# First layer: modulation weights worked feature by feature, with the first three projection tiles accumulated alongside

## The chip, the cores and the metric

One core of a Trainium2 chip runs the whole program; the other cores are idle. The number that counts is the device time of one execution in microseconds. PE is TensorE (matmuls), DVE is VectorE, ACT is ScalarE, POOL is GpSimd, and SP issues most of the loads. Each engine works through its own list of instructions in order and waits for the others by semaphores, so an instruction that waits holds up everything behind it on its engine.

## What is computed

Two layers of a diffusion backbone on 256 latent and 256 context tokens, 1024 features wide. Cut to the part that the change touches:

```python
silu_c, silu_cc = silu(c), silu(c_ctx)                 # conditioning vectors, 1024 each
for l in range(2):
    mx = silu_c @ w_ada[l] + b_ada[l]                  # (6 * 1024): shift, scale, gate, twice
    mc = silu_cc @ w_ada[l] + b_ada[l]                 # the same for the context tokens
    sh1, sc1, ga1, sh2, sc2, ga2 = split(mx, 6)
    ux = (rmsnorm(x, g_mix[l]) * (1 + sc1) + sh1) @ w_in[l]
    # uc the same from ctx and mc; then four token mixers, one output projection,
    # x = x + ga1 * (...), and a second modulated norm with a SwiGLU (layer 1: 8 experts)
```

The change is in the opening of layer 0: how `sh1` and `sc1` (the first 2048 of the 6144 modulation features, from an 8 MB slice of `w_ada[0]`) are made, and when the projection by `w_in[0]` begins.

## The kernel before, in words

Activations lie with features on the partitions: `xt[k]` is feature tile k (128 features) by 512 tokens (256 latent, 256 context). The program runs in stages. They are an opening, the mixer of layer 0 (projections, then attention and two other mixers, then the output projection `w_out`), a dense feed-forward, the mixer of layer 1 and the experts.

**Opening.** `ada_first` (L166 to L193) loads the 8 MB slice as 16 tiles of 512 KB, each 128 of the 1024 inputs by 1024 of the 2048 outputs. Every output needs all inputs, so two accumulators (`pss`) take 64 small matmuls (L179, 32 rows by 256 columns, the operand being silu of the two conditioning vectors), and no feature is known before the last tile is in. Between them stand the loads of `xt`, their squares and sum (`add_sq`, tile `sm`), and `spread` (L195), which copies the conditioning vectors over all partitions (tile `scb`) by 16 matmuls on 16 little tiles that DVE makes. `inv_rms` turns `sm` into the reciprocal norms `rs`, which stay in a PSUM tile of the pair named S. Then four transposes (L189) bring the features onto partitions, as `mod[0]`.

**Modulated input.** `modulated` (L269) makes `A` (gain times one plus scale) for all tiles at once, and then for each k: DVE makes `ht`, ACT the rounded high part `hh[k]` (L286) and the shifted sum (L288, second half of the tokens), DVE and POOL the low part `hl[k]` (L291 and L289).

**Projections.** Each product is three matmuls per feature tile, L135 to L137: high by high, low by high, high by low, 24 for one output tile of 512 columns. The weights come through `pump` (L97): a `raw` load on SP, the high part on ACT (L102), the low part alternately on POOL and DVE (L104). Twelve projections (`proj`) and a transposed pair make the mixer's inputs; three PSUM accumulators named acc rotate among them, and one is free again when ACT has copied and squared what is in it.

**Columns.** The other 4096 features of layer 0, and all of layer 1, come otherwise: `more(n)` takes n columns `ar` (512 KB, two buffers) and DVE multiplies each by `scb` and sums it, once per conditioning vector (L227). `more` is called after every `proj` with the number of its output tiles, twice in the transposed pair, and once in each of four attention calls. `w_out` (L557) then works off what is missing: it may begin its first tile only with at most 62 of the 80 columns left, and it ends only with 56 left, since the dense stage needs those.

The order on each engine is set by a scheduler that goes by readiness; the columns' instructions keep the order of the program among themselves (`pinned`).

Of the kernel before, what the change touches and what calls it, by code (L numbers as in the profile page):

```python
# [52 lines left out]
def backbone(ctx: ExitStack, tc: tile.TileContext, a: dict, out: bass.AP, dbg=None):  # L53
# [10 lines left out]
    def acc(w=512):  # L64
        return psp.tile([128, 512], F32, name="acc", bufs=3)[:, :w]
# [98 lines left out]
    def ada_first():  # L164

        pss = [acc(256) for _ in range(2)]  # L166
        sm = per.tile([128, T], F32, name="sm", bufs=2)
        for k in range(KT):
            if k == 2:
                spread()  # L170
            for hf in range(2):
                if 2 <= k < 6:
                    i = 2 * k + hf - 4
                    sp.dma_start(xt[i], a["xt"][i])
                    add_sq(sm, i, T)
                r = wa.tile([128, 1024], F32, name="wa", bufs=6)
                sp.dma_start(r, a["wa0"][k, hf])
                for g in range(4):
                    pe.matmul(pss[hf][32 * g:32 * g + 32], scv[:, k, :], r[:, 256 * g:256 * g + 256],  # L179
                              start=k == 0, stop=k == KT - 1)  # L180
            if k == 5:
                table(AF.Sqrt, sm)
        rs = at_once(inv_rms(sm, T, 128, D))
        for hf in range(2):
            ev = per.tile([128, T], F32, name="sq", bufs=2)[:, :256]
            (dve.tensor_copy if hf else act.copy)(ev, pss[hf])
            for c in range(2):
                pm = psp.tile([128, 512], F32, name="T", bufs=2)[:, :128]
                pe.transpose(pm, ev[:, 128 * c:128 * c + 128], C("ident"))  # L189
                m = mod[0][:, 8 * hf + c:8 * hf + 8:2]  # L190
                bias = V(0, "b_ada", 8 * hf, 8)[:, c::2]
                dve.tensor_add(m, pm.rearrange("p (g z) -> p g z", g=4)[:, :, :2], bias[:, :, None].to_broadcast([128, 4, 2]))
        return rs  # L193
# [75 lines left out]
    def modulated(l, gname, jsh, jsc, tmp, w, sm, emit, then=None, rs=None, nt=3):  # L269
        A = tmp.tile([128, KT, 2], F32, name="A")  # L270
        for s in range(w // 256):
            dve.scalar_tensor_tensor(A[:, :, s], mod[l][:, jsc:jsc + KT, s], 1.0, V(l, gname, 0, 8), op0=ALU.add, op1=ALU.mult)
        if rs is None:
            rs = at_once(inv_rms(sm[:, :w], w, 128, D))
        if then:
            table(then, rs)
        for k in range(KT):
            t = tmp.tile([128, T], F32, name="ht", bufs=nt)
            for s in range(w // 256):
                c = slice(256 * s, 256 * s + 256)  # L280
                dve.scalar_tensor_tensor(t[:, c], xt[k][:, c], A[:, k, s:s + 1], rs[:, c], op0=ALU.mult, op1=ALU.mult)
                emit(k, s, c, t, mod[l][:, jsh + k, s:s + 1])

# [10 lines left out]
    def mixer(l, sm, oh, ol, rs=None):  # L294
# [5 lines left out]
        mx = ctx2.enter_context(sb(f"mx{l}"))  # L300
        qh = [mx.tile([96, nx], F32, name=f"qh{h}") for h in range(4)]
        kh = [mx.tile([96, T], F32, name=f"kh{h}") for h in range(4)]
        nq = [mx.tile([128, nx], F32, name=f"nq{h}") for h in range(2)]
        nk = [mx.tile([128, T], F32, name=f"nk{h}") for h in range(2)]
        vv = mx.tile([128, 4, 256], F32, name="vv")
        nv = mx.tile([128, 4, 256], F32, name="nv")
        rf = [mx.tile([128, nx], F32, name=f"rf{i}") for i in range(2)]
        rp = [mx.tile([128, nx], F32, name=f"rp{i}") for i in range(2)]
        nb = mx.tile([128, 2, 4, 256], F32, name="nb")
        swb = mx.tile([128, 768], F32, name="swb")  # L310
        cstc = mx.tile([128, 1280], F32, name="cstc")
        wf = swb[:, :512].rearrange("p (k c) -> p k c", k=2)
        wp = swb[:, 512:].rearrange("p (k c) -> p k c", k=2)
        g8 = mx.tile([128, 1], F32, name="g8")
        dve.tensor_scalar(g8, V(l, "g_naq"), 0.125, None, op0=ALU.mult)
        with sb(f"hp{l}", "right") as hp:
# [7 lines left out]
            pump(2 if last else 3)  # L324
# [4 lines left out]
            modulated(l, "g_mix", 0, 8, hp, T, sm, emit, None, rs, nt)  # L329
# [95 lines left out]
            p, p1 = proj(2, T)  # L425
            spawn(keys(p))
            spawn(rope(p1, T, V(l, "g_kr"), kh))
            spawn(queries(proj(2, nx)))
# [919 lines left out]
    act.activation(scv[:, :, :2], cv, AF.Silu)  # L1348
    rxp = None
# [10 lines left out]
    with ExitStack() as early:  # L1360
        adp = early.enter_context(sb("adp"))
        with sb("wa", "right") as wa:
            rs = ada_first()
        pump(0)
        with ExitStack() as ctx2:
            sm = mixer(0, None, None, None, rs)
# [80 lines left out]
def _layout(i):  # L1447
# [8 lines left out]
    d["wa0"] = wa[0, :, :2048].reshape(KT, 128, 2, 1024).transpose(0, 2, 1, 3)  # L1456
# [78 lines left out]
```

## Time and profile before

| | |
|---|---|
| three runs | 1800.61, 1801.84, 1802.29 us (median 1801.84) |
| profiled execution | 1801.68 us, of which 1799.9 us span |
| PE busy | 1638.6 us, 91% of the span |
| DVE busy | 831.1 us, 46% |
| ACT busy | 573.8 us, 32% |
| POOL busy | 384.0 us, 21% |
| HBM read | 472.76 MB, 263 GB/s over the span |
| mean granted PE clock | 0.954 of full speed |

The busy shares are averages over stages with different limits, so they do not tell what a change in the opening is worth. For that one reads the opening, the projections and `w_out` one by one: which engine works in each, and which wait ends last. PE's busy time is modelled to the end of each pipelined matmul; the distance from one start to the next says how fast it really goes.

### The profile page before, as it was taken

The page shows a single profiled execution, that of the slowest core. Times are in us where ns is not written, and L with a number is a line of the kernel's source. Part 1 is how long each engine was busy: PE and PEld are TensorE (multiplying, and loading weights), DVE is VectorE, ACT ScalarE, POOL GpSimd, SP SyncE. Part 2 cuts the span into 40 slices and gives each one's busy share as a digit, 9 for nine tenths or more (in the row PEclk, how much of TensorE's full clock was granted, in tenths as well). Part 3 has the DMA queues.
Part 4 walks back from the last instruction along what each step waited for, and adds up shares of the span by engine and source line. Part 5 has one row for each costly group of instructions (what it writes and reads, how often), then busy time and mean ns, then how long its engine had stood idle before and what let it go on. Part 6 is the DMA issues. An engine that isn't in the chain of part 4 may idle for free. (4 is left out here: it accounts for less than half of the span.)

```text
span 1799.9 us, 21849 instructions
## 1 busy us (share of the span) xinstructions
PE 1638.6 (91%) x8330; PEld 1062.4 (59%) x8330; DVE 831.1 (46%) x1336; ACT 573.8 (32%) x922; POOL 384.0 (21%) x210
## 2 busy tenths in 40 slices
PE   5999998999999999998988759999988979989986
PEld 2786576888888878775343235555553357753422
DVE  3759887666565654563020024434432068830101
ACT  3433534232222235452010123434420057720100
POOL 0413014444444434221000001212210014410000
PEclk8899998999999999998999969999999989999999
DMA  8634143544447763526999945889878999979997
GB/s 297 211 94 141 48 129 105 166 150 153 140 146 241 235 222 117 200 82 247 420 417 419 417 166 234 350 333 363 355 281 320 420 403 362 362 280 419 417 420 296
DMA packets 84619, 476.11 MB, mean 265 GB/s; under 512 B 9808, under 2 KB 10832, under 8 KB 41168
## 3 DMA queue, kind: packets, MB, share of 16 engines
q1 hardware_dynamic: 80976, 459.84, 67.2%
q10 hardware_dynamic: 2592, 7.71, 1.2%
q0 software_dynamic: 864, 6.29, 0.9%
q8 instruction: 89, 1.46, 0.3%
q14 instruction: 98, 0.80, 0.1%
HBM read 472.76 MB, written 1.05 MB: 263 GB/s over the span
## 5 line engine op out<-in xcount | busy, mean ns | idle before, releaser
L900 PE MATMUL acc<-slot,xe 128*64 128x512 f32 x1120 | 274.7, 632 | 55.9 <-DMA slot<-in_wm 31.0
L104 POOL TENSOR_TENSOR wlo<-raw,whi 128x1024 fp32r<-128x1024 f32 (+1 forms) x87 | 213.4, 2453 | 427.9 <-ACT whi L102 394.6
L1041 POOL TENSOR_TENSOR wl<-slot,wh 128x1024 fp32r<-128x1024 f32 x42 | 103.4, 2462 | 656.5 <-ACT wh L1039 656.5
L1041 DVE TENSOR_TENSOR wl<-slot,wh 128x1024 fp32r<-128x1024 f32 x126 | 182.9, 1476 | 130.7 <-ACT wh L1039 128.7
L900 PEld LDWEIGHTS acc<-slot,xe 128*64 128x64 f32 x1120 | 96.2, 144 | 201.7 <-issue 189.3
L102 ACT ACTIVATE whi<-raw 128x1024 fp32r<-128x1024 f32 (+1 forms) x112 | 116.8, 1045 | 305.0 <-PE acc L136 198.5
L1039 ACT CAST wh<-slot 128x1024 fp32r<-128x1024 f32 x168 | 176.1, 1053 | 118.5 <-PE acc L900 79.0
L1110 DVE SCALAR_TENSOR_TENSOR sq<-sq,gs,acc 64x512 f32<-64x512 f32 (+1 forms) x53 | 39.7, 750 | 345.0 <-ACT sq L1109 339.0
L135 PE MATMUL acc<-fhh,whi 128*128 128x512 f32 x352 | 137.4, 393 | 1.7 <-ACT fhh L286 1.7
L136 PE MATMUL acc<-fhl,whi 128*128 128x512 f32 x352 | 137.9, 392 | 0.0
L137 PE MATMUL acc<-fhh,wlo 128*128 128x512 f32 x352 | 137.6, 391 | 0.0
L900 PE MATMUL acc<-wh,xr 128*128 128x512 f32 x400 | 131.2, 410 | 6.5 <-issue 3.9
L227 DVE SCALAR_TENSOR_TENSOR ar<-ar,scb 128x1024 f32<-128x1024 f32 x80 | 115.0, 1437 | 28.8 <-DMA ar<-in_waT 27.1
L900 PEld LDWEIGHTS acc<-wh,xr 128*128 128x128 f32 x400 | 73.4, 192 | 41.0 <-issue 22.4
L900 PE MATMUL acc<-wl,xr 128*128 128x512 f32 x200 | 79.9, 399 | 0.0
L135 PE MATMUL acc<-hh,whi 128*128 128x512 f32 (+1 forms) x192 | 71.4, 378 | 6.4 <-ACT hh L286 6.4
L135 PEld LDWEIGHTS acc<-fhh,whi 128*128 128x128 f32 x352 | 66.6, 190 | 16.0 <-ACT fhh L286 2.1
L1109 ACT ACTIVATE sq<-acc 64x512 f32<-64x512 f32 (+1 forms) x56 | 33.0, 589 | 132.4 <-PE acc L900 132.4
L136 PEld LDWEIGHTS acc<-fhl,whi 128*128 128x128 f32 x352 | 66.5, 189 | 14.6 <-POOL fhl L289 0.9
L137 PEld LDWEIGHTS acc<-fhh,wlo 128*128 128x128 f32 x352 | 66.6, 189 | 13.6
L900 PE MATMUL S<-slot,scv 128*64 128x512 f32 x320 | 72.5, 594 | 0.0
L136 PE MATMUL acc<-hl,whi 128*128 128x512 f32 (+1 forms) x192 | 71.1, 371 | 0.7 <-POOL hl L289 0.6
(305 smaller groups left out, 2749.7 us busy)
## 6 DMA issues: line engine op xcount, KB each, us to landing
slot<-in_wm SPq DMA_DIRECT2D x330, 1024.0 KB, 14.8
ar<-in_waT SPq DMA_DIRECT2D x80, 512.0 KB, 3.7
raw<-in_w SPq DMA_DIRECT2D x44, 512.0 KB, 3.6
raw<-in_win SPq DMA_DIRECT2D x28, 512.0 KB, 4.1
wa<-in_wa SPq DMA_DIRECT2D x16, 512.0 KB, 7.1
raw<-in_wout SPq DMA_DIRECT2D x16, 512.0 KB, 4.2
raw<-in_w2d SPq DMA_DIRECT2D x16, 512.0 KB, 4.2
slot<-in_wm POOLq DMA_DIRECT2D x6, 1024.0 KB, 11.1
```

The source lines that it names most:

```text
L102: act.activation(hi[:, :n], r[:, :n], AF.Copy)
L104: (pool if low[0] % low_every == 0 else dve).tensor_sub(lo[:, :n], r[:, :n], hi[:, :n].bitcast(F32))
L135: pe.matmul(ps, w[0], x[0], start=first, stop=False)
L136: pe.matmul(ps, w[0], x[1], start=False, stop=False)
L137: pe.matmul(ps, w[1], x[0], start=False, stop=last)
L227: i = dve.scalar_tensor_tensor(o, r, 1.0, scb[:, s], op0=ALU.mult, op1=ALU.mult, accum_out=mod[l][:, j, s:s + 1])
L900: return pe.matmul(o, l, r, start=first, stop=last_)
L1039: group("act", lambda hi=hi, src=src: act.copy(hi, src), [], [f"hi{r}"], [i])
L1041: group(en, lambda en=en, hi=hi, lo=lo, src=src: eng[en].tensor_sub(lo, src, hi.bitcast(F32)), [f"hi{r}"], [f"lo{r}"], [i])
L1109: group("act", lambda: act.activation(y[P], h1, AF.Silu), [], [hn[0], f"gg{g}"])
L1110: group("dve", lambda: dve.scalar_tensor_tensor(y[:128 - P.start], y[P], gs[P, gc + u:gc + u + 1], h3, op0=ALU.mult, op1=ALU.mult), [f"gs{ ...
```

## The change

1. The 8 MB slice is laid out by the features that it produces: 8 tiles of 1 MB, tile k holding all 1024 inputs for the 128 shift and the 128 scale features of feature tile k. Three buffers hold them.
2. `ada_first` is gone. `first_input` loads `xt` first and sums the squares. `ada_pair(k)` loads a tile, runs 8 small matmuls into a PSUM tile of the pair S, lets ACT copy it (`ev`), and with two matmuls against a 128 by 2 selector (`pick2`) gets shift and scale of feature tile k, which one DVE addition puts into `mod[0]`.
3. `modulated` takes a generator `each` and makes `A` for one k at a time.
4. `begin` splits three `win` chunks outside `pump` (ACT high part, POOL low part for all three) and after each `hh[k]`, `hl[k]` runs `part`: the nine matmuls of feature tile k for the first three output tiles, which stay in the three acc accumulators. The mixer's first `proj(2)` and half of the second are then left out, and with them three calls of `more`.
5. `spread` moves from the opening behind that loop.
6. The mixer's tiles (`mx`) are made after the loop, in memory that the loop's tiles had.

```diff
+    def ada_pair(wa, k):
+        r = wa.tile([128, KT, 256], F32, name="wa", bufs=3)
+        sp.dma_start(r, a["wa0"][k])
+        yield
+        q = aux(256)
+        for i in range(KT):
+            g = 32 * (i % 4)
+            pe.matmul(q[g:g + 32], scv[:, i, :], r[:, i], start=i < 4, stop=i >= 4)
+        ev = wa.tile([128, 256], F32, name="ev", bufs=2)
+        act.copy(ev, q)
+        p = psp.tile([128, 512], F32, name="T", bufs=2)[:, :4]
+        for i in range(2):
+            pe.matmul(p[:, 2 * i:2 * i + 2], ev[:, 128 * i:128 * i + 128], pick2, start=True, stop=True)
+        bias = V(0, "b_ada", k, 9)[:, ::8]
+        dve.tensor_add(mod[0][:, k:k + 9:8], p.rearrange("p (h s) -> p h s", h=2), bias[:, :, None].to_broadcast([128, 2, 2]))
...
+            def begin():
+                with sb("wa") as wa:
+                    steps = [ada_pair(wa, k) for k in range(KT)]
+                    ws = []
+                    for i in range(3):
+                        if i < 2:
+                            next(steps[i])
+                        r, _ = raw(todo.pop(0))
+                        w = [wa.tile([128, 1024], F32R, name=f"w{n}{i}") for n in "hl"]
+                        act.activation(w[0], r, AF.Copy)
+                        pool.tensor_sub(w[1], r, w[0].bitcast(F32))
+                        ws.append(w)
+                    ps = [acc() for _ in range(3)]
+                    for k in range(KT):
+                        if k + 2 < KT:
+                            next(steps[k + 2])
+                        next(steps[k], 0)
+                        yield
+                        if k:
+                            part(ps, ws, k - 1)
+                        if k in (4, 6):
+                            pump(k - 4)
+                    yield
+                    part(ps, ws, KT - 1)
+                    begun.extend(ps)
+                    spread()
+                yield
...
-            p, p1 = proj(2, T)
+            p, p1 = begun[:2] or proj(2, T)
             spawn(keys(p))
             spawn(rope(p1, T, V(l, "g_kr"), kh))
-            spawn(queries(proj(2, nx)))
+            spawn(queries(begun[2:] + proj(1, nx) if begun else proj(2, nx)))
...
-    d["wa0"] = wa[0, :, :2048].reshape(KT, 128, 2, 1024).transpose(0, 2, 1, 3)
+    d["wa0"] = wa[0, :, :2048].reshape(KT, 128, 2, KT, 128).transpose(3, 1, 0, 2, 4).reshape(KT, 128, KT, 256)
```

How the lists of the engines change, at three places. First PE around the first projection. The names are those of the code with a buffer number; wh and wl are the split chunks, scv the conditioning vectors. Before, all small matmuls come first:

```order
L179 MATMUL acc_98<-wa_272,scv_73 32x256 x4
L189 MATMUL T_299<-cst_61,sq_297 128x128
L179 MATMUL acc_99<-wa_278,scv_73 32x256 x4
L189 MATMUL T_307<-cst_61,sq_305 128x128
L135 MATMUL acc_462<-hh0_347,whi_365 128x512
L135 MATMUL acc_463<-hh0_347,whi_371 128x512
L136 MATMUL acc_462<-hl0_355,whi_365 128x512
L137 MATMUL acc_462<-hh0_347,wlo_366 128x512
```

and now, in one turn of the loop (k = 2):

```order
L181 MATMUL S_290<-wa_218,scv_73 32x256 x8
L135 MATMUL acc_189<-hh2_134,wh0_171 128x512
L135 MATMUL acc_190<-hh2_134,wh1_179 128x512
L135 MATMUL acc_191<-hh2_134,wh2_185 128x512
L186 MATMUL T_301<-pick2_85,ev_299 128x2 x2
L136 MATMUL acc_189<-hl2_142,wh0_171 128x512
L137 MATMUL acc_189<-hh2_134,wl0_172 128x512
L136 MATMUL acc_190<-hl2_142,wh1_179 128x512
L137 MATMUL acc_190<-hh2_134,wl1_180 128x512
L136 MATMUL acc_191<-hl2_142,wh2_185 128x512
L137 MATMUL acc_191<-hh2_134,wl2_186 128x512
L181 MATMUL S_325<-wa_253,scv_73 32x256 x8
```

The small matmuls of the next feature tile now stand ahead of each group of nine, and its selector pair inside it.

Second ACT at the end of the loop, up to the first release of an accumulator (`ckv`, `rw` and `cq0` are copies of the three). Before, the copy and the square of the first accumulator stand together:

```order
L286 ACTIVATE hh7_354<-ht_442,mod0_71 128x256 x2
L288 ACTIVATE ht_442<-ht_442,mod0_71 128x256
L431 DMA nb_339<-in_nab 128x2048
L102 ACTIVATE whi_456<-raw_375 128x1024
L338 COPY ckv_522<-acc_462 128x512
L343 ACTIVATE sq_524<-acc_462 128x512
```

and now:

```order
L102 ACTIVATE whi_581<-raw_434 128x1024
L199 COPY scb_90<-S_484 128x512
L286 ACTIVATE hh7_139<-ht_458,mod0_71 128x256 x2
L288 ACTIVATE ht_458<-ht_458,mod0_71 128x256
L378 COPY ckv_573<-acc_189 128x512
L378 COPY rw_577<-acc_190 128x512
L378 COPY cq0_634<-acc_191 128x512
L199 COPY scb_90<-S_498 128x512
L471 DMA nb_562<-in_nab 128x2048
L199 COPY scb_90<-S_512 128x512
L199 COPY scb_90<-S_526 128x512
L383 ACTIVATE sq_575<-acc_189 128x512
```

The copies out of the moved `spread` (`scb`) now stand between the copy and the square of the first accumulator, and one of them ahead of `hh7`.

Third DVE at the first tile of `w_out` (`xt_63` is feature tile 0, mod the modulation, ar a column). Before:

```order
L227 SCALAR_TENSOR_TENSOR sq,mod_71<-ar,scb 128x1024
L227 SCALAR_TENSOR_TENSOR ar,mod_71<-ar,scb 128x1024
L567 SCALAR_TENSOR_TENSOR xt_63<-acc,mod_71,xt_63 128x256
L230 TENSOR_SCALAR mod_71<-mod_71,vec 128x2
L567 SCALAR_TENSOR_TENSOR xt_63<-acc,mod_71,xt_63 128x256
```

and now:

```order
L222 SCALAR_TENSOR_TENSOR sq,mod_71<-ar,scb 128x1024
L222 SCALAR_TENSOR_TENSOR ar,mod_71<-ar,scb 128x1024
L607 SCALAR_TENSOR_TENSOR xt_63<-acc,mod_71,xt_63 128x256
L225 TENSOR_SCALAR mod_71<-mod_71,vec 128x2
L222 SCALAR_TENSOR_TENSOR sq,mod_71<-ar,scb 128x1024
L607 SCALAR_TENSOR_TENSOR xt_63<-acc,mod_71,xt_63 128x256
L222 SCALAR_TENSOR_TENSOR ar,mod_71<-ar,scb 128x1024
L104 TENSOR_TENSOR wlo<-raw,whi 128x1024
```

From the last attention output to the reciprocal norm of the dense stage, DVE's list held 8 columns (pairs of L227) and 3 weight splits (L104); it now holds 11 columns and 4 splits. Ahead of attention it held 13 columns and now holds 10.

## Rows read from the trace of the kernel before

**Rows 1.** The page: span and number of instructions.
```profile
span 1799.9 us, 21849 instructions
```

**Rows 2.** Load rate, first 60 us in 40 slices of 1.5 us.
```profile
GB/s 0 114 297 413 426 415 415 392 400 404 407 397 397 145 49 266 253 333 337 392 412 421 418 418 404 175 255 160 0 0 11 248 407 363 25 0 14 240 180 330
```

**Rows 3.** Opening in time order: start us, us, engine, line, out<-in, count, [idle before <-releaser].
```profile
31.05 1.87 PE L247 MATMUL T<-cst,sm 128*128 128x1 f32 x8 [1.76 <-DVE sm L239]
32.85 1.93 PE L179 MATMUL acc<-wa,scv 128*32 128x256 f32 x16
...
34.71 1.12 PE L259 MATMUL S<-cst,rr 128*128 128x128 f32 x4
...
40.29 2.34 POOL L104 TENSOR_TENSOR wlo<-raw,whi 128x1024 fp32r<-128x1024 f32 x1 [39.86 <-ACT whi L102]
...
43.62 1.04 ACT L102 ACTIVATE whi<-raw 128x1024 fp32r<-128x1024 f32 x1
...
45.11 1.22 PE L135 MATMUL acc<-hh,whi 128*128 128x512 f32 x2 [4.88 <-ACT hh L286]
```

**Rows 4.** Granted clock: one window, columns PE, PEld, DVE, ACT, POOL, PEclk, DMA, GB/s.
```profile
40.00:50.00 10.00, 4.54 (x11) 2.93 (x10) 9.81 (x18) 5.22 (x12) 4.67 (x3) 0.56 0.47 166
```

**Rows 5.** Timeline, first projection tiles: matmuls at either clock, modulated input.
```profile
49.21 0.63 PE L136 MATMUL acc<-hl,whi 128*128 128x512 f32 x1
...
49.53 0.86 DVE L281 SCALAR_TENSOR_TENSOR ht<-xt,A,S 128x256 f32<-128x256 f32 x2
...
49.64 0.63 PE L137 MATMUL acc<-hh,wlo 128*128 128x512 f32 x1
...
50.06 0.89 ACT L286 ACTIVATE hh<-ht,mod 128x256 fp32r<-128x256 f32 x2
...
51.43 0.74 POOL L289 TENSOR_TENSOR hl<-ht,hh 128x256 fp32r<-128x256 f32 x1 [0.46 <-ACT ht L288]
...
53.05 0.40 PE L136 MATMUL acc<-hl,whi 128*128 128x512 f32 x1
...
53.28 0.39 PE L137 MATMUL acc<-hh,wlo 128*128 128x512 f32 x1
```

**Rows 6.** Timeline, spread: two of its 16 little tiles on DVE.
```profile
16.31 0.28 DVE L202 TENSOR_SCALAR sq<-cst,scv 128x128 f32<-128x128 f32 x1 [0.21 <-PE S L203]
...
17.48 0.28 DVE L202 TENSOR_SCALAR sq<-cst,scv 128x128 f32<-128x128 f32 x1 [0.21 <-PE S L203]
```

**Rows 7.** Timeline on PE: the fourth tile's last matmul and the fifth's first.
```profile
72.52 0.40 PE L137 MATMUL acc<-hh,wlo 128*128 128x512 f32 x1
...
73.54 0.48 PE L135 MATMUL acc<-hh,whi 128*128 128x512 f32 x1
```

**Rows 8.** Timeline, PE and DVE at a gap in the sixth tile.
```profile
81.51 2.83 DVE L393 TENSOR_TENSOR sq<-sq 128x512 f32<-128x512 f32 x1
...
84.39 1.05 PE L247 MATMUL T<-cst,sq 128*128 128x1 f32 x8 [2.42 <-DVE sq L393]
...
85.63 0.61 PE L136 MATMUL acc<-hl,whi 128*128 128x512 f32 x1
...
89.02 0.41 PE L135 MATMUL acc<-hh,whi 128*128 128x512 f32 x1
```

**Rows 9.** The stage of w_out: one window, then DVE and PE in time order.
```profile
238.80:287.40 48.60, 42.46 (x189) 34.07 (x187) 45.09 (x71) 15.15 (x20) 14.66 (x5) 0.96 0.52 163
...
259.50 1.22 DVE L227 SCALAR_TENSOR_TENSOR sq<-ar,scb 128x1024 bf16<-128x1024 f32 x1
...
262.17 0.87 DVE L567 SCALAR_TENSOR_TENSOR xt<-acc,mod,xt 128x256 f32<-128x256 f32 x2
262.96 1.21 DVE L104 TENSOR_TENSOR wlo<-raw,whi 128x1024 fp32r<-128x1024 f32 x1
...
278.12 3.30 DVE L227 SCALAR_TENSOR_TENSOR ar<-ar,scb 128x1024 f32<-128x1024 f32 x1
...
287.45 1.86 PE L247 MATMUL T<-cst,sm 128*128 128x1 f32 x8 [6.19 <-DVE sm L239]
```

More of the change, by code (lines that the diff above doesn't have):

```diff
@@ L161, in later, with first_input @@
         dve.tensor_copy(t[:, 0:1], x[:, 0:1].bitcast(F32))
-    def ada_first():
-        pss = [acc(256) for _ in range(2)]
+    def first_input():
         sm = per.tile([128, T], F32, name="sm", bufs=2)
         for k in range(KT):
[L169 to L193, printed above, removed]
@@ new lines, in first_input @@
+            sp.dma_start(xt[k], a["xt"][k])
+            add_sq(sm, k, T)
+        table(AF.Sqrt, sm)
+        return sm
+    def ada_pair(wa, k):
[13 more added lines that the diff above has]
+        dve.tensor_add(mod[0][:, k:k + 9:8], p.rearrange("p (h s) -> p h s", h=2), bias[:, :, None].to_broadcast([128, 2, 2]))
@@ L267, in at_once, with modulated @@
                 return e.value
-    def modulated(l, gname, jsh, jsc, tmp, w, sm, emit, then=None, rs=None, nt=3):
+    def modulated(l, gname, jsh, jsc, tmp, w, sm, emit, then=None, nt=3, each=None):
         A = tmp.tile([128, KT, 2], F32, name="A")
[L271 to L274, printed above, removed]
+        if not each:
+            for s in range(w // 256):
+                dve.scalar_tensor_tensor(A[:, :, s], mod[l][:, jsc:jsc + KT, s], 1.0, V(l, gname, 0, 8), op0=ALU.add, op1=ALU.mult)
+        rs = at_once(inv_rms(sm[:, :w], w, 128, D))
         if then:
@@ L277, in modulated @@
         for k in range(KT):
+            if each:
+                next(each)
+                dve.tensor_scalar(A[:, k], mod[l][:, jsc + k], 1.0, V(l, gname, k), op0=ALU.add, op1=ALU.mult)
             t = tmp.tile([128, T], F32, name="ht", bufs=nt)
@@ L282, in modulated @@
                 emit(k, s, c, t, mod[l][:, jsh + k, s:s + 1])
+        if each:
+            next(each)
     def shifted(hh, hl, k, s, c, t, sh):
@@ L291, in shifted, with mixer @@
             dve.scalar_tensor_tensor(lo, t, sh, hi.bitcast(F32), op0=ALU.add, op1=ALU.subtract)
-    def mixer(l, sm, oh, ol, rs=None):
+    def mixer(l, sm, oh, ol):
         nonlocal cstb, rxp
@@ L299, in mixer @@
         nst = 1 if last else 2
[L300 to L315, printed above, removed]
         with sb(f"hp{l}", "right") as hp:
@@ L323, in mixer @@
             cstb = hp.tile([128, 1024], F32, name="cstb")
-            pump(2 if last else 3)
+            if last:
+                pump(2)
             def emit(k, s, c, t, sh):
                 shifted(hh, hl, k, s, c, t, sh)
-            modulated(l, "g_mix", 0, 8, hp, T, sm, emit, None, rs, nt)
+            def begin():
[25 more added lines that the diff above has]
+                yield
@@ new lines, in part @@
+            def part(ps, ws, k):
+                c = slice(128 * k, 128 * k + 128)
+                for p, (whi, wlo) in zip(ps, ws):
+                    mm3(p, (whi[:, c], wlo[:, c]), (hh[k], hl[k]), k == 0, k == KT - 1)
+            begun = []
+            opening = None if last else begin()
+            modulated(l, "g_mix", 0, 8, hp, T, sm, emit, None, nt, opening)
+            if opening:
+                next(opening)
+            mx = ctx2.enter_context(sb(f"mx{l}"))
+            qh = [mx.tile([96, nx], F32, name=f"qh{h}") for h in range(4)]
@@ new lines, in mixer @@
+            kh = [mx.tile([96, T], F32, name=f"kh{h}") for h in range(4)]
+            nq = [mx.tile([128, nx], F32, name=f"nq{h}") for h in range(2)]
+            nk = [mx.tile([128, T], F32, name=f"nk{h}") for h in range(2)]
+            vv = mx.tile([128, 4, 256], F32, name="vv")
+            nv = mx.tile([128, 4, 256], F32, name="nv")
+            rf = [mx.tile([128, nx], F32, name=f"rf{i}") for i in range(2)]
+            rp = [mx.tile([128, nx], F32, name=f"rp{i}") for i in range(2)]
+            nb = mx.tile([128, 2, 4, 256], F32, name="nb")
@@ L330, in mixer @@
+            swb = mx.tile([128, 768], F32, name="swb")
+            cstc = mx.tile([128, 1280], F32, name="cstc")
+            wf = swb[:, :512].rearrange("p (k c) -> p k c", k=2)
+            wp = swb[:, 512:].rearrange("p (k c) -> p k c", k=2)
+            g8 = mx.tile([128, 1], F32, name="g8")
+            dve.tensor_scalar(g8, V(l, "g_naq"), 0.125, None, op0=ALU.mult)
             act.dma_start(swa, a["sw"][l, :, :1280])
@@ L1348, in backbone @@
     act.activation(scv[:, :, :2], cv, AF.Silu)
+    pick2 = per.tile([128, 2], F32, name="pick2")
+    dve.reduce_sum(pick2, C("ident").rearrange("p (g z) -> p z g", g=4)[:, :2], axis=AX.X)
     rxp = None
@@ L1361, in backbone @@
         adp = early.enter_context(sb("adp"))
-        with sb("wa", "right") as wa:
-            rs = ada_first()
-        pump(0)
+        sm = first_input()
         with ExitStack() as ctx2:
-            sm = mixer(0, None, None, None, rs)
+            sm = mixer(0, sm, None, None)
         if dbg:
```

## The prediction, made before the changed kernel ran

> **What bounds the kernel now.** I read the page first, then the waits of PE, then the stages that the change touches. The span is 1799.9 us [rows 1] in an execution of 1801.68 us, so 1.8 us lie outside it, and the runs' median is 1801.84 us. Behind the opening PE works nearly without a break, so time won or lost ahead of the dense stage should reach the end unchanged. From there on both programs have the same columns left and the same lists but for names and for which of two engines makes a low part.
>
> The opening ends at 45.11 us, when the first projection matmul starts after a wait of 4.88 us [rows 3]. Its loads run at some 400 GB/s up to 19.5 us and then with holes [rows 2]; the granted clock is 0.56 around its end [rows 4], which is nearly the lower of PE's two levels, 1.2 GHz. A matmul of 512 columns then starts every 0.43 us; at full clock every 0.23 us [rows 5]. Three output tiles are 72 of these, 16.7 us at full clock. That is the most that working them alongside the loads could take off.
>
> Two later places matter. In the sixth tile PE waits 2.42 us for a DVE addition that stands behind two columns, and then goes slowly until 89.02 [rows 8]. In the stage of w_out DVE is busy 45.09 of 48.60 us, and PE then waits 6.19 us for its last sum [rows 9]: this stage is DVE's.
>
> **The opening, part by part.** Queue order and the load rate give the arrivals. The slices up to 4.5 us move 0.62 MB, later ones 0.41 MB per us [rows 2]. Constants and xt are 2.7 MB: 9.6 us. swa and cstb are now issued early by ACT (1.2 MB) and share with the first weight tile (1 MB): 14.7 us. A chunk of w_in (0.5 MB) takes 1.3 us and a weight tile 2.6 us, in SP's order: chunk 0 at 16.3, tile 1 at 18.9, chunk 1 at 20.2, chunk 2 at 21.4, tile 2 at 24.0. The sum of squares, paced by the arrivals, ends near 11; from there to the broadcast norm it took 4.8 us (31.05 to 34.71 plus 1.12) [rows 3], so that comes near 16 and is not what is waited for.
>
> What is waited for is POOL. It now makes the low parts of all three chunks, 2.34 us each, behind ACT's high parts at 1.04 us [rows 3], and hl0 stands behind them in its list. Chunk 1 at 20.2 gives its high part at 21.3 and low part at 23.7; the third low part ends at 26.1, and hl0 with 0.74 us [rows 5] and some contention near 27.0. Before it PE does the three high products and stops.
>
> From 27 on PE has work. It starts at the lower clock; in the rows it came up 4.6 us after the gap at 84.39 [rows 8] and at most 7.9 us after 45.11 [rows 3, 5]. I take 5.5. Six matmuls (2.6), eight small ones (1.93 at that clock [rows 3]) and two more (0.9) bring PE to 32.4; at full clock a selector pair (0.5, for which the norm's eight records in 1.87 us at the lower clock are the nearest row [rows 3]) and seven matmuls (1.6) to 34.5.
>
> A turn at full clock costs PE eight small matmuls (1.1, with half of 1.93 and the fill), a pair (0.5) and nine at 0.23: 3.7 us. The chain around the turn is as long: from ht to hh 1.42 us (49.53 to 50.95), two more steps of ACT at about 0.45, as each hh takes [rows 5], the pair, and four hand-overs with two small DVE steps, which I put at 0.8, make 3.6 us. So the turn is hidden by nothing and hides little; loads at 2.6 us a tile do not limit it. Four turns, k = 2 to 5: 49.3.
>
> Turns 6 and 7 are longer, because the pump and spread come in. Behind ev6 (near 47.6) ACT has two high parts of 1.04 us around the halves of hh6, POOL a low part of 2.34 us ahead of hl6: 54.0 instead of about 51. Then four matmuls, the last small eight and the pair: 57.1. Between there and hh7 stand four of spread's tiles, a high part and a copy: hh7 at 60.3, hl7 at 61.6, six matmuls: 63.0.
>
> Behind the loop spread is no longer covered. In the opening of before it lay beside loads. DVE may fill the mixer's new tiles only when the loop's memory is free (63.0), and its last eight tiles stand behind that, one per 0.6 us [rows 6]: 68.7 with the last two matmuls. ACT copies two results ahead of the square that frees the first accumulator: 70.0. The bounds for this uncovered piece are 3 us (ten matmuls at 0.28, as the four of 1.12 us [rows 3]) and 8 us. The fourth tile takes 24 at 0.23, 75.6, and the norm pair behind it 1.8: **77.4**. In before, the same work is done when the fourth tile's last matmul has started, 72.52 plus 0.23 [rows 7]. The opening loses **4.7 us**, with bounds of 8 us gained (nothing on PE waits behind 27) and 10 lost.
>
> **The projections.** Three calls of more are gone, and the addition that PE waited for now stands ahead of any column in DVE's list. That wait (2.42) and the slow matmuls behind it (eight in 3.39 us, 85.63 to 89.02, instead of 1.86) [rows 8] go: **3.9 us gained**, at least nothing. What is late next is the first softmax, where DVE's last columns stand in the same order as before, so I count nothing there.
>
> **w_out.** The three columns come back here, since the stage may not end with more than 56 left. A column takes 2.67 us of DVE (259.50 to 262.17), a further split 1.21 [rows 9]. DVE has 45.1 us to do and gets 8.0 and 1.2 more; of its 3.5 us of idle time I keep 1.4, for the chain of the last tile. That is 55.7 instead of 48.6: **7.1 us lost**. Behind each waiting column in DVE's list stand the additions to xt that free PE's accumulators, so PE stops, and the dense stage begins later. Below, 3 us, if PE's waits leave DVE room; above, 10.
>
> One row shows a column pass of 3.30 us where its partner took 1.22 [rows 9], beside a subtraction on POOL. The Trainium skill's page "GPSIMD Engine Reference", section "Specifications", says that POOL shares its SBUF interfaces with VectorE, with contention for instructions with two SBUF inputs; a column is one. If each added column met POOL, the stage would lose 6 us more, and the time would be 1816.
>
> **Sum.** 4.7 - 3.9 + 7.1 = 7.9 us; 1801.68 + 7.9 = 1809.6, against the median 1809.7. I predict 1809.5.
>
> **Rivals.** *The loop hides the opening* (faster). If POOL's low parts come earlier or the clock is up by 27, and PE never waits in turns 6, 7 and spread, PE's list alone takes 37.8 us from 27 at full clock (93 matmuls 21.6, six small eights 6.6, six pairs 3, spread 4.8, norms 1.8): the fourth tile and its norms are done at 64.8, a gain of 8. Then -8 - 3.9 + 7.1 = -4.8: 1797. It decides at the point where hl0 is ready below 25 us or the last piece of spread costs under 3 us. For it: of the 50.4 us from 27 to 77.4 in my count 12.6 are waits and slow clock, spread over many small links. Against: the subtraction times and the lists above. 0.18.
>
> *w_out takes the columns without loss* (no change). If the added columns fill DVE's idle time ahead of w_out and PE's tail of 6.19 us, the stage loses 0 to 2: 1803. For it: 3.5 us of idle time in the stage. Against: 45 of 48.6 us are taken. 0.18.
>
> *The clock stays low in the loop* (slower still). At the lower level a turn is 6.7 us instead of 3.7; four turns and the two long ones would cost some 14 us more: 1823. The Trainium skill, "TensorE: Matmul & The Clock Gate", section "HAM oscillation — how this bites in real kernels", says that pauses between short groups of matmuls bring the lower clock back for every group, which speaks against splitting the projection this way. Against the rival: at the lower clock the turn is all PE's work, so PE would not pause, and the clock rose in such work from 45.11 to 53.05 [rows 3, 5]. 0.08.
>
> **How the numbers follow.** My forecast has 0.56, its own range 1805.5 to 1816. The range over the cases is 1796.5 to 1820: it leaves out most of the last rival and a little below. A measurement of this kernel tells about 0.2% (3.6 us) from no change. Slower by more: the forecast and the last rival, 0.64. Within: 0.19. Faster: 0.17.
>
> **What would show it.** The first hl0 product near 27 us, turns of 3.7 us from the mid thirties, the loop's last product near 63, an idle-looking PE with spread up to about 70, and the fourth tile's end near 76. No wait for the queries' sum in the projections. In w_out, 11 columns, DVE without gaps, and PE's wait for the last sum longer than 6.19 us or waits for accumulators in the middle. I am wrong if the fourth tile ends below 70, or if w_out is as long as before.

## The result, and the profile of the changed kernel

The changed kernel takes 1829.48 us (median; 1828.91 to 1830.09) against 1801.43 us for the kernel before on the same chip: ratio 1.0156, 95% interval 1.0138 to 1.0173. It is 28 us slower; 1809.5 us was predicted. The page of the profiled execution begins:

```profile
span 1827.4 us, 21900 instructions
```

Against [rows 1] that is 27.5 us more. Landmarks on PE, read from both timelines, tell where they arise (us; the last column is what the stage that ends there adds):

| landmark | before | changed | behind by | added |
|---|---|---|---|---|
| fifth tile's first matmul | 73.54 | 77.71 | 4.2 | 4.2 |
| eighth tile's first matmul | 105.65 | 104.79 | -0.9 | -5.0 |
| first attention scores | 157.70 | 165.41 | 7.7 | 8.6 |
| first w_out product | 230.21 | 244.26 | 14.1 | 6.3 |
| first dense product | 292.71 | 311.01 | 18.3 | 4.3 |
| end of the dense stage | 657.92 | 676.75 | 18.8 | 0.5 |
| first expert product | 833.85 | 857.73 | 23.9 | 5.1 |
| end of the experts' products | 1791.25 | 1818.06 | 26.8 | 2.9 |

**Opening** (answers to [rows 3, 5, 7]). Timeline of the changed kernel, in time order; the columns are start us, us, engine, line, operation, out<-in, shapes, count, [idle before <-releaser]:

```profile
28.08 0.80 PE L136 MATMUL acc<-hl,wh 128*128 128x512 f32 x1 [2.19 <-POOL hl L289]
...
49.67 1.22 DVE L104 TENSOR_TENSOR wlo<-raw,whi 128x1024 fp32r<-128x1024 f32 x1
...
50.93 2.57 POOL L104 TENSOR_TENSOR wlo<-raw,whi 128x1024 fp32r<-128x1024 f32 x1 [2.96 <-ACT whi L102]
...
54.24 0.50 PE L136 MATMUL acc<-hl,wh 128*128 128x512 f32 x1 [1.97 <-POOL hl L289]
...
63.49 0.50 PE L136 MATMUL acc<-hl,wh 128*128 128x512 f32 x1 [0.55 <-POOL hl L289]
...
70.31 0.50 PE L135 MATMUL acc<-hh,whi 128*128 128x512 f32 x1 [1.18 <-ACT sq L383]
...
76.01 1.84 PE L242 MATMUL T<-cst,sq 128*128 128x1 f32 x16
```

The first hl0 product starts at 28.08, the turns from 34.74 on are 3.76 us apart, hl6 waits for POOL's low part at 50.93, the fourth tile starts at 70.31, and the norm products behind it start at 76.01.

**Projections** (answers to [rows 8]). The wait in the sixth tile is gone. Three new ones stand ahead of the eighth tile's first matmul and behind that tile, and the granted clock falls after the first two; timeline on PE, then two windows (columns as in [rows 4]):

```profile
104.79 0.50 PE L135 MATMUL acc<-hh,whi 128*128 128x512 f32 x1 [0.53 <-ACT sq L383]
...
118.48 1.05 PE L242 MATMUL T<-cst,sq 128*128 128x2 f32 x8 [0.85 <-ACT sq L383]
...
148.14 0.63 PE L254 MATMUL S<-cst,rx 128*128 128x128 f32 x4 [1.62 <-DVE rx L249]
```
```profile
108.00:112.00 4.00, 4.00 (x15) 3.18 (x14) 0.00 (x0) 0.00 (x0) 0.00 (x0) 0.80 0.00 0
120.00:124.00 4.00, 4.00 (x24) 4.00 (x23) 0.49 (x2) 0.39 (x2) 0.00 (x0) 0.59 0.45 131
```

The eighth tile takes 7.4 us (104.79 to 112.20) where it took 5.8 (105.65 to 111.48).

**First softmax.** Before, PE waited 3.04 us there; now 8.01, because DVE comes to the first maximum only at 174.84, 9.4 us after the first scores; before, it came 5.3 us after them. Timeline of the kernel before, two rows, and of the changed kernel:

```profile
162.99 1.29 DVE L485 TENSOR_REDUCE m<-acc 128x1 f32<-128x512 f32 x2
...
165.20 1.13 PE L480 MATMUL acc<-kh,qh 96*128 96x512 f32 x2 [3.04 <-ACT pr L488]
```
```profile
156.20 2.64 DVE L222 SCALAR_TENSOR_TENSOR sq<-ar,scb 128x1024 bf16<-128x1024 f32 x1 [2.02 <-DMA ar<-in_waT]
...
166.35 1.23 DVE L222 SCALAR_TENSOR_TENSOR sq<-ar,scb 128x1024 bf16<-128x1024 f32 x1 [2.53 <-DMA ar<-in_waT]
...
166.50 3.27 POOL L104 TENSOR_TENSOR wlo<-raw,whi 128x1024 fp32r<-128x1024 f32 x1 [8.74 <-PE acc L520]
...
167.62 3.24 DVE L222 SCALAR_TENSOR_TENSOR ar<-ar,scb 128x1024 f32<-128x1024 f32 x1
...
170.79 1.21 DVE L104 TENSOR_TENSOR wlo<-raw,whi 128x1024 fp32r<-128x1024 f32 x1
...
174.84 0.69 DVE L525 TENSOR_REDUCE m<-acc 128x1 f32<-128x512 f32 x1
...
176.59 2.08 PE L520 MATMUL acc<-kh,qh 96*128 96x512 f32 x2 [8.01 <-ACT pr L528]
```

DVE waits twice for a column's load, one column pass beside POOL's subtraction takes 3.24 instead of 1.2 us, and a low part and a column follow, all ahead of the maximum.

**w_out** (answers to [rows 9]). One window each from the first w_out product to the first dense product, the kernel before and the changed one:

```profile
230.21:292.71 62.50, 54.03 (x243) 41.30 (x241) 49.84 (x87) 21.01 (x35) 14.66 (x5) 0.93 0.46 144
```
```profile
244.26:311.01 66.75, 55.95 (x249) 42.08 (x247) 55.79 (x101) 21.49 (x35) 12.19 (x4) 0.92 0.48 158
```

The last wait of the stage in the changed kernel (before, it was 6.19 us, [rows 9]):

```profile
305.74 1.86 PE L242 MATMUL T<-cst,sm 128*128 128x1 f32 x8 [7.81 <-DVE sm L234]
```

DVE has 11 columns instead of 8 and 5.95 us more to do; the stage is 4.25 us longer.

**Second mixer.** The change does not touch its code. One window each from the end of the dense stage to the experts, before and changed, and the timelines at two places:

```profile
657.92:833.85 175.93, 163.78 (x1051) 134.87 (x1050) 96.86 (x231) 87.07 (x179) 54.26 (x58) 0.96 0.44 157
...
658.97 1.22 DVE L104 TENSOR_TENSOR wlo<-raw,whi 128x1024 fp32r<-128x1024 f32 x1
...
660.69 0.69 DVE L239 TENSOR_TENSOR sm<-sm,sq 128x512 f32<-128x512 f32 x1 [0.51 <-ACT sq L238]
...
661.44 1.05 PE L247 MATMUL T<-cst,sm 128*128 128x1 f32 x8 [1.83 <-DVE sm L239]
...
716.69 2.38 POOL L104 TENSOR_TENSOR wlo<-raw,whi 128x1024 fp32r<-128x1024 f32 x1
```
```profile
676.75:857.73 180.98, 166.35 (x1052) 137.04 (x1050) 97.67 (x231) 87.02 (x179) 55.88 (x58) 0.94 0.42 152
...
678.17 2.35 POOL L104 TENSOR_TENSOR wlo<-raw,whi 128x1024 fp32r<-128x1024 f32 x1
...
679.52 1.56 DVE L234 TENSOR_TENSOR sm<-sm,sq 128x512 f32<-128x512 f32 x1 [1.64 <-ACT sq L233]
...
681.14 1.87 PE L242 MATMUL T<-cst,sm 128*128 128x1 f32 x8 [2.70 <-DVE sm L234]
...
737.24 3.18 POOL L410 TENSOR_TENSOR qh<-rw,ht 32x256 f32<-32x256 f32 x3
738.38 1.45 DVE L104 TENSOR_TENSOR wlo<-raw,whi 128x1024 fp32r<-128x1024 f32 x1
...
741.22 0.37 ACT L378 COPY rw<-acc 128x256 f32<-128x256 f32 x1 [2.79 <-POOL qh L410]
...
742.09 0.61 PE L242 MATMUL T<-cst,sq 128*128 128x2 f32 x4 [2.18 <-ACT sq L383]
```

In the kernel before, the first low part was DVE's (658.97) and the second POOL's (716.69). Each is now made by the other engine: POOL's lies beside DVE's sum, which takes 1.56 instead of 0.69 us, and DVE's beside POOL's rotation, for which ACT waits. PE then waits 2.70 instead of 1.83 us at the first place and 2.18 us anew at the second; the rest of the 5.1 us is PE's busy time, 166.35 instead of 163.78 us at a granted clock of 0.94 instead of 0.96.

### The profile page after: what moved, and what is told of

The parts are those of the page before. It is cut to its first block, busy times and chain, and to the rows that moved or that the text cites. A ratio compares the mean times of both kernels' runs of the same rounds, so it can differ in the third digit from the quotient of the medians.

```text
span 1827.4 us, 21900 instructions
## 1 busy us (share of the span) xinstructions
PE 1643.7 (90%) x8358; PEld 1065.9 (58%) x8358; DVE 819.4 (45%) x1345; ACT 577.1 (32%) x929; POOL 386.7 (21%) x211
## 5 line engine op out<-in xcount | busy, mean ns | idle before, releaser
L940 PE MATMUL acc<-slot,xe 128*64 128x512 f32 x1120 | 269.8, 625 | 58.5 <-DMA slot<-in_wm 38.3
L104 POOL TENSOR_TENSOR wlo<-raw,whi 128x1024 fp32r<-128x1024 f32 (+1 forms) x85 | 207.6, 2443 | 399.7 <-ACT whi L102 360.6
L222 DVE SCALAR_TENSOR_TENSOR sq<-ar,scb 128x1024 bf16<-128x1024 f32 x48 | 68.5, 1428 | 4.6 <-DMA ar<-in_waT 4.5
L135 PE MATMUL acc<-gh,whi 128*128 128x512 f32 x176 | 69.8, 396 | 0.0
## 6 DMA issues: line engine op xcount, KB each, us to landing
slot<-in_wm POOLq DMA_DIRECT2D x6, 1024.0 KB, 10.8
```

The costliest lines, as they stand in the source:

```text
L104: (pool if low[0] % low_every == 0 else dve).tensor_sub(lo[:, :n], r[:, :n], hi[:, :n].bitcast(F32))
L135: pe.matmul(ps, w[0], x[0], start=first, stop=False)
L222: i = dve.scalar_tensor_tensor(o, r, 1.0, scb[:, s], op0=ALU.mult, op1=ALU.mult, accum_out=mod[l][:, j, s:s + 1])
L940: return pe.matmul(o, l, r, start=first, stop=last_)
```

## The experiments

The kernel before was run again beside each group, at 1800.9, 1803.0 and 1802.7 us.

**The counter.** The low parts are dealt to POOL and DVE in turn by a counter. The three tiles of the opening bypass it; three is odd.

```diff
-    low = [0]
+    low = [3]
```

> The changed kernel with one number different: the counter that deals the low parts of the weights to DVE and POOL in turn starts at 3, so that the fourth and every later tile's low part is made by the engine that made it in the kernel before. Theory P (the three tiles that the opening takes past the counter leave it odd, so in both mixers every later low part falls to the other engine and meets other work there): the 2.18 us wait for ACT's squares and the 2.70 us wait for DVE's sum in the second mixer go, the first softmax is reached behind one column fewer on DVE so that its wait falls from 8.0 to about 3 us, and the time falls by 10 to 17 us, to 1812 to 1819. Theory C (the three columns that fell away ahead of the attention are what costs) expects less than 2 us of change: 1828 to 1831. Theory S (the spread at the opening's end) expects no change.

Measured: 1818.64 us (ratio 1.0097, 1.0079 to 1.0115), 10.8 below the changed kernel. The second mixer takes 175.69 us, as before the change. The stage from the attention scores to w_out takes 71.71 instead of 78.85 us (before: 72.51): a low part of DVE's and POOL's swap, one column fewer stands on DVE between the first scores and the maximum, and the wait is 2.24 us. That is 12.4 us. The projections gain nothing: from the eighth tile to the attention it takes 61.13 us, in the changed kernel 60.62. Part was lost again in the opening, where POOL instead of DVE now makes a low part; beside it a small DVE step ahead of hh6 takes 2.40 us, and PE waits 3.63 instead of 1.45 us for hh6:

```profile
49.59 2.38 POOL L104 TENSOR_TENSOR wlo<-raw,whi 128x1024 fp32r<-128x1024 f32 x1 [0.60 <-ACT whi L102]
49.59 2.40 DVE L275 TENSOR_SCALAR A<-mod,vec 128x2 f32<-128x2 f32 x1
...
54.50 1.65 PE L135 MATMUL acc<-hh,wh 128*128 128x512 f32 x3 [3.63 <-ACT hh L286]
```

The clock then stayed low longer (0.56 in 64 to 68 us, 1.00 in the changed kernel), and the fourth tile came at 76.30. The same flip in the kernel before:

```diff
-    low = [0]
+    low = [1]
```

> The kernel before with one number different: the counter that deals the low parts to DVE and POOL starts at 1, so every low part of both mixers is made by the other engine; nothing else is changed. Theory P: the second mixer becomes 4 to 5 us longer with the waits that the changed kernel shows there, the first mixer 0 to 12 us longer: 1806 to 1818. Theories C and S: within 2 us of the kernel before, 1800 to 1804.

Measured: 1807.5 us, ratio 1.0036 (1.0024 to 1.0049). Up to the dense stage it is 1.0 us behind; the loss lies in the second mixer (same window as above):

```profile
658.97:841.51 182.54, 167.99 (x1051) 139.02 (x1050) 98.32 (x231) 86.89 (x179) 55.96 (x58) 0.93 0.42 151
```

So the flip costs the second mixer 5 to 7 us in either program, but the 7 us in the first attention only in the changed one; there this kernel loses 1.9. From the eighth tile to the attention it takes 52.05 us as before, so the flip is not what crowds the projections. Over all kernels of this study the second mixer takes 175.7 to 178.5 us in the seven that deal its low parts as before and 180.5 to 182.8 in the seven that deal them the other way. Set right for the second mixer alone:

```diff
-        low_every = 2
+        low_every = 2; low[0] += 1
```

> The changed kernel with the counter set right by one behind the dense stage only, so that the low parts fall to the engines of the kernel before in the second mixer alone. Theory P for the second mixer: everything up to 676 us as in the changed kernel, the three waits there go, and the time falls by 5 to 6 us, to 1823 to 1825. If the flip costs there less than the profile of the changed kernel says: above 1826.

Measured: 1824.66 us, 4.8 below the changed kernel and inside the expected range; the window:

```profile
681.70:857.73 176.03, 163.76 (x1050) 134.80 (x1050) 96.89 (x231) 87.33 (x179) 54.20 (x58) 0.96 0.44 157
```

The window shows the cause; that the total fits as well is in part chance. Up to the end of the dense stage this program is the changed kernel, yet its profiled execution comes there at 681.70 instead of 676.75 us (opening 1.6 later, attention stage 82.16 instead of 78.85 us), and it makes this up in the experts' stage (954.9 instead of 960.3 us). So one execution of the same code can be some 5 us from another by the dense stage, and a stage's difference of 2 or 3 us in one profile shows little by itself.

**The columns.** Three calls of more behind the opening:

```diff
-            p, p1 = begun[:2] or proj(2, T)
+            more(3 * bool(begun)); p, p1 = begun[:2] or proj(2, T)
```

> The changed kernel with three more column calls directly behind the opening, where DVE has little to do; as in the kernel before, 13 column calls then stand ahead of the attention and 7 are left for the stage of w_out. Theory C: the stage of w_out (244.26 to the dense stage at 311.01) gets shorter by its 4.3 us, and the wait at the first softmax with it: 1818 to 1825. Theory P: the second mixer's waits and the first softmax's stay as they are; only the stage of w_out moves, by at most 4 us: 1825 to 1829. Theory S: no change.

Measured: 1828.44 us (1818.46 to 1830.92): no clear gain, and its four executions span 12 us. In the profiled one w_out has 8 columns again and takes 61.74 us, 5 less; but the opening ran at clock 0.50 from 56 to 68 us and the eighth tile came at 110.50. Theory C is right on w_out and nowhere else. The same columns taken away from the kernel before:

```diff
-                more(n)
+                more(n - skip.pop() if skip else n)
...
-            p, p1 = proj(2, T)
+            skip = [] if last else [1, 2]; p, p1 = proj(2, T)
```

> The kernel before with three column calls fewer in its first tiles, as the changed kernel has it, and nothing else changed: 10 calls ahead of the attention, 10 in the stage of w_out. Theory C: the stage of w_out becomes 4 to 5 us longer, all else stays: 1805 to 1807 against 1801 to 1803. If the columns are hidden in w_out: within 1.5 us of the kernel before.

Measured: 1805.75 us (1796.8 to 1809.21), ratio 1.0011 (0.9997 to 1.0026). w_out, by its window, is 4.85 us longer than before, as theory C says:

```profile
226.26:293.61 67.35, 55.89 (x244) 42.33 (x242) 56.71 (x102) 21.12 (x35) 14.09 (x5) 0.93 0.49 157
```

Not expected: the eighth tile comes at 98.85 instead of 105.65 us. Of these 6.8 us 2.4 lie ahead of the fifth tile (71.17 instead of 73.54), where the two programs are the same: the first projection product came earlier in this execution, at 43.15 instead of 45.11:

```profile
43.15 1.22 PE L135 MATMUL acc<-hh,whi 128*128 128x512 f32 x2 [4.99 <-ACT hh L286]
```

The other 4.4 are the columns': without the three the sixth tile has no wait. So moving three columns from the projections to w_out is worth 4.4 us at one end and costs 7.7 by the dense stage (2.9 in the attention stage, 4.85 in w_out); the total is not clear of noise. All columns out of the projections, in the changed kernel:

```diff
-                more(n)
+                n * last and more(n)
...
-                more(1)
+                last and more(1)
```

> The changed kernel without column calls from the opening to the attention; they are all left to the stage of w_out, which becomes some 25 us longer, so the total says nothing and only the projections are read. Theory D (columns on DVE, beside the low parts on POOL, hold up squares and norms in the eighth tile and behind it): the waits of 0.53, 0.85 and 1.62 us go, the clock stays up, and the attention starts 5 to 7 us earlier than at 165.41, about 159 us. Rival (the chains themselves come a step later, columns or not): the attention starts at 164 to 166 us.

Measured: 1849.49 us, as the stage of w_out has 22 columns. The attention starts at 160.79, 4.6 us earlier than in the changed kernel, though the eighth tile comes 1.3 later. From the eighth tile to the attention it takes 54.74 us where the changed kernel takes 60.62 and the kernel before 52.05; these three windows, and that of the kernel before with three columns fewer:

```profile
106.05:160.79 54.74, 54.72 (x317) 45.96 (x317) 17.80 (x32) 18.49 (x34) 13.60 (x8) 1.00 0.22 66
```
```profile
104.79:165.41 60.62, 58.12 (x315) 48.63 (x316) 36.97 (x61) 18.29 (x34) 15.44 (x8) 0.94 0.25 85
```
```profile
105.65:157.70 52.05, 52.05 (x300) 44.08 (x300) 39.88 (x62) 17.60 (x30) 17.07 (x8) 1.00 0.38 119
```
```profile
98.85:150.90 52.05, 52.05 (x300) 44.03 (x300) 39.89 (x62) 17.60 (x30) 17.08 (x8) 1.00 0.39 120
```

All three waits are gone and the clock stays at 1.00, so these 5.9 us go with the columns (theory D); their loads are gone with them, and the run does not tell the two apart. The amount of DVE's work is not the reason, since both versions of the old opening have more of it here (39.9 us against 37.0) and no wait. The other 2.7 are PE's own: about 16 more records. Four of them are products of one chain (`acc<-swa,ckv`) that start at 126.69 in the changed kernel and, ahead of the eighth tile, at 100.50 before.

**The spread** at the opening's front:

```diff
-                    ps = [acc() for _ in range(3)]
+                    ps = [acc() for _ in range(3)]; spread()
...
                     begun.extend(ps)
-                    spread()
```

> The changed kernel with the spread of the conditioning vector moved from the opening's end to its front, ahead of the first modulation product, where PE waits for weights. Theory S: the fourth tile starts at about 66.5 instead of 70.31 us, and the time falls by 3.5 to 4 us, to about 1825.5; if it delays the first product of the low half beyond 28.1 us, half of that. Theories P and C see nothing in it beyond those 4 us: 1825 to 1830.

Measured: 1831.74 us (1828.64 to 1835.41), no gain. Its tiles on DVE lie beside POOL's three low parts, PE is at the spread until 30.89, and the first modulation product starts 15 us later than in the changed kernel:

```profile
31.57 1.94 PE L181 MATMUL S<-wa,scv 128*32 128x256 f32 x16 [0.68 <-ACT scb L199]
```

The turns then run almost without a wait, and the fourth tile starts at 70.00 us all the same: the spread was paid for ahead of the loop instead of behind it.

**The loop without splits** (hi written once by DVE from hl7 ahead of ACT's copy; pump(2) behind the last part):

```diff
+            behind and dve.tensor_copy(hi[:, 0:1], behind[:, 256:257])
...
-                        if k in (4, 6):
-                            pump(k - 4)
+                        if k == 4:
+                            pump(0)
...
-                    part(ps, ws, KT - 1)
+                    part(ps, ws, KT - 1); pump(2, hl[KT - 1])
```

> The changed kernel with the first two splits behind the three tiles kept out of the opening loop: their high parts wait, through a one-element copy on DVE, for the loop's last low part; the loads stay where they were. Theory L (in turns 6 and 7 POOL and DVE make these low parts ahead of hl6, PE waits 1.45 and 1.97 us and its clock falls): both turns take 3.8 us, the loop's last product ends near 58 instead of 65.15 us, the clock does not fall, and the fourth tile starts at 64 to 66 instead of 70.31 us: the time falls by 4 to 6 us, to 1823 to 1826. Rival: the splits now stand in the way of the spread, and the fourth tile starts at 69 to 71 us as before: 1828 to 1831.

Measured: 1830.52 us, no gain. hl6 waits only 0.45 us and the loop ends at 63.15 instead of 65.15, but now the spread stands behind the low parts on DVE:

```profile
67.46 0.75 PE L198 MATMUL S<-sq,cst 128*128 128x128 f32 x4 [2.99 <-DVE sq L197]
...
72.14 0.79 PE L135 MATMUL acc<-hh,whi 128*128 128x512 f32 x1 [1.18 <-ACT sq L383]
```

**Steps of the chains,** two rounds behind the opening:

```diff
             spawn(rope(p1, T, V(l, "g_kr"), kh))
+            begun and advance(); begun and advance()
```

> The changed kernel with two rounds of steps for the waiting chains directly behind the opening, which the pair of tiles gave in the kernel before. Theory A (the chains of keys and rotations stand a step or two later against the tiles, so that their squares, sums and norms crowd the end of the projections): the waits of 0.53, 0.85 and 1.62 us in the eighth tile and behind it go, and the low clock after two of them with them; the attention starts 4 to 7 us earlier than at 165.41 us: 1821 to 1826. Rival: the crowd is made by columns and low parts on DVE and POOL, the waits only move: 1828 to 1831.

Measured: 1829.59 us; the attention starts at 168.37, later than before the edit. The opening of this execution ran slower (the last products of the spread start at 71.82 instead of 68.42), but from there to the attention it takes 96.6 us, in the changed kernel 97.0, where 4 to 7 us of gain were expected. Theory A falls: the three waits are gone, and new ones of 0.66 and 0.75 us stand ahead of earlier tiles.

**Together:** the loop without splits, the counter at 3 and the three columns; then with the steps as well; then, instead of the steps, with the spread and the three columns behind the fourth tile:

```diff
                     begun.extend(ps)
-                    spread()
...
-            more(3 * bool(begun)); p, p1 = begun[:2] or proj(2, T)
+            p, p1 = begun[:2] or proj(2, T)
...
             spawn(queries(begun[2:] + proj(1, nx) if begun else proj(2, nx)))
+            begun and (spread(), more(3))
```

> Three edits at once: the clean loop (as in the run that keeps the splits out of it), the counter starting at 3, and the three columns behind the opening. If the three causes add up: 11 us from the counter, 5 from the loop and some 4 from the columns, 1807 to 1811. If the columns give nothing: 1812 to 1815. If the counter's gain came from the longer opening of its run (76.3 us to the fourth tile): above 1818.

Measured: 1812.86 us (1812.22 to 1814.86), ratio 1.0060 (1.0041 to 1.0079). The attention stage takes 71.70 us, w_out 62.49 and the second mixer is back: the loss that is left is brought along from ahead of the attention, from the opening and the projections: 11.0 us at its start, 10.2 at the first dense product.

> The three edits and the two rounds of steps. By theory A some 5 us below the run with three edits, 1801 to 1807; by its rival no change against it.

Measured: 1817.82 us; the steps cost 5 us.

> The kernel with three edits (clean loop, counter at 3, three columns), with the spread written behind the fourth tile, so that its small matmuls stand inside the fourth and fifth tile and nothing waits for it. Theory S (the spread between loop and fourth tile is uncovered): the fourth tile starts at 65 to 67 instead of 72.21 us, the spread costs PE 2.4 us inside the tiles, and the time falls by 3 to 5 us against 1812.9, to 1808 to 1810. Rival: the fourth tile waits as long for the freed accumulator and the split: 1812 to 1814.

Measured: 1816.09 us, slower than either theory had it. The fourth tile does start at 63.48 us, 8.7 earlier than with three edits, but spread and columns then hold up DVE in the next tiles, and the attention starts 3 us later:

```profile
98.03 1.05 PE L242 MATMUL T<-cst,sq 128*128 128x2 f32 x8 [3.04 <-ACT sq L383]
```

No version was faster than the kernel before.

## Why the prediction was right in direction and wrong in size

1. *Opening: lost 4.7 expected, 4.2 measured.* Most links held: hl0 27.0 (28.08), turns 3.7 (3.76), hl6 54.0 (54.24), loop end 63.0 (65.15), first accumulator freed 70.0 (70.31), fourth tile's end 75.6 (76.0). One made up for another: hl0 came 1.1 us late, but the matmuls were slow behind it for 2.9 us, not 5.5. The clock, low again around 57 us (0.74, 0.50 and 0.90 in the 2 us from 54, 56 and 58), is most of the difference in the last turn. The opening's price against the kernel before with three columns fewer, which has the old opening and as many columns, is 5.9 us at the eighth tile (104.79 against 98.85), 2.4 of them that execution's early start.
2. *Gap in the sixth tile: gained 3.9 expected, 5.0 measured.* The reason was right, columns ahead of an addition; it is a gift of the three calls, and the old opening gets 4.4 us of it too.
3. *"I count nothing there": this is the step that failed.* I took it that DVE's last columns stand in the same order as before. They don't. Two things were missing. From the eighth tile to the attention it cost 8.6 us: the chains stand later against the tiles, which brings 2.7 us of moved work, and 5.9 us that go with the columns. From the attention to w_out it cost 6.3 us: the counter had changed which low parts are DVE's, and setting it right gives 7.1 back. What counts there is how far DVE is with its list when the scores come: in the changed kernel and the four flipped versions that share its long wait the first maximum comes 9.2 to 9.8 us behind the first scores, in the flipped old program 3.6, in the flipped run with the steps 4.2.
4. *w_out: lost 7.1 expected, 4.3 and 4.9 measured.* The term was right and too large: DVE's busy time rose by 5.95 us, not 9.2, since fewer passes were stretched beside POOL (8 columns 25.8 us before, 3.2 each, three passes stretched; 11 columns 30.8 after, 2.8 each, two stretched). Every profiled kernel with 8 columns there takes 61.7 to 62.5 us for the stage, every one with 11 takes 66.8 to 67.4.
5. *From the dense stage on "the same lists but for names and for which of two engines makes a low part".* I saw the difference and priced it at nothing. It is 5.1 us by the trace, 4.8 by the run that sets it right there alone.
6. The last 2.9 us, in the experts' stage, are not explained: from the first expert product to the end of the experts' products the kernels of this study take 952.9 to 960.3 us with the same code, so it may be scatter.

Steps 1, 2 and 4 sum to 3.5 us where I had 7.9; the rest of the 28 us is steps 3 and 5 (about 20) and the remainder of stages I did not price. So the direction was luck in part: the measured sum of what I had priced, 3.5 us, is no more than the 3.6 us that I had put down as noise. The rival with the low clock came true in small: not in the loop's steady turns, but at its end, in the eighth tile, and in some of the experiments' openings. The Trainium skill's "TensorE: Matmul & The Clock Gate", section "HAM oscillation — how this bites in real kernels", warns of pauses between groups of matmuls. The trace agrees only in part: the clock was 0.80 in 108 to 112 us, behind a pause of 0.53 us, but 1.00 behind pauses of 1.18 us (ahead of 70.31) and 1.62 us (ahead of 148.14):

```profile
70.00:74.00 4.00, 3.69 (x16) 3.01 (x17) 0.00 (x0) 0.75 (x2) 0.00 (x0) 1.00 0.99 387
```
```profile
148.00:152.00 4.00, 3.86 (x19) 3.25 (x20) 4.00 (x4) 0.87 (x1) 2.24 (x1) 1.00 0.19 43
```

What decides between the two is not shown here.

What stays open: why the projections with the new opening crowd more than in the kernel before with three columns fewer, which has as many. Steps, spread and splits were moved one at a time and none removed it; only taking the columns away did, and with them their loads. The 10 us that are left with three edits were not brought down further.

## What to carry to other kernels

When a change makes work bypass a counter or a queue that deals out later work, follow the deal to the end of the program: a shift by an odd number cost 5 us in a stage whose code was not touched. On an engine that is busy for most of a stretch, an edit that frees the waiting engine mostly moves the wait: price what the next wait would be, by what that engine still has to do before it. And time one part alone in the old program, as was done here with the counter and the three columns. Read a stage over several kernels that share it: two executions of one program lay 5 us apart by the dense stage, while the second mixer and w_out fall into two clean groups each.

## What the runs showed of the hardware

A pass over a column takes 1.21 to 1.23 us alone. Where a POOL subtraction had begun before it, it took up to 3.45 us and in several rows ended some 1.1 us after the subtraction did, as if it had waited for it (167.62 to 170.86 beside 166.50 to 169.77). Where the pass had begun first, it kept its 1.22 us, and the subtraction took 3.26 to 3.42 us (four rows of the changed kernel) instead of the 2.35 to 2.57 of most rows. A DVE step of only 128x2 took 2.40 us beside a subtraction, else 0.23. The Trainium skill's "GPSIMD Engine Reference", section "Specifications", names the SBUF interfaces that POOL shares with VectorE; the trace agrees, and adds that the one that begins second loses nearly all that is left of the other. TensorE's granted clock fell after single waits of 0.53 and 0.85 us that followed steady work, to 0.80 and 0.59 in the windows shown, and did not after single waits of 1.18 and 1.62 us. In the opening it was 0.50 from 56 to 68 us in the kernel with three more columns, where the changed kernel, with the same order on PE and DVE up to there, had 0.70 from 56 to 60 and then 1.00.
